# Mixture-of-experts kernel: the block for crowded experts moved ahead of the fourth expert from the end, and gathered columns computed transposed, 192 at once

## The chip, the cores and the metric

The kernel runs on one core of a Trainium2 chip. The metric is device time in microseconds of one execution. A core has five engines with queues of their own: PE (TensorE, matrix products into PSUM), DVE (VectorE), ACT (ScalarE), POOL (GpSimd) and SP (SyncE, which here issues the DMAs). They meet through semaphores.

## The reference, cut to what matters

One encoder layer on 256 tokens of width 1024: three token mixers (attention, a state-space scan, a convolution), a merge, a LayerNorm, then 32 experts, of which each token uses four, and a last LayerNorm. All in float32. The part around the change is the mixture of experts:

```python
logits = t @ router_w + router_b                    # t: 256 x 1024, normalised
top_vals, top_idx = lax.top_k(logits, 4)            # of 32 experts
gates = softmax(top_vals)
# for each expert e, on the tokens that chose it:
h = xe @ w_gu[e] + b_gu[e]                          # 1024 -> 2048
gate, up = minimum(h[:, :1024], 7), clip(h[:, 1024:], -7, 7)
y = ((up + 1) * (gate * sigmoid(1.702 * gate))) @ w_dn[e] + b_dn[e]   # 1024 -> 1024
# output: sum over the token's experts of gate * y; then
x = layernorm(2**0.25 * x + ffn, ln2_g, ln2_b)
```

The weights of the experts, 32 x 12 MB in float32, are read once from HBM.

## The kernel before, in words

**Weights.** Each expert has twelve tiles of 1 MB: eight of `w_gu` (the "up" tiles, one for each 128 rows, index k) and four of `w_dn` (the "down" tiles). They go through a ring of 19 slots in SBUF, in the order of use (`load`, L746 to L751, all on SP's queue). A slot is loaded again when its reader on PE is done. The first 19 tiles are loaded during the mixers, as space comes free (`do_pre`, `open_ring`).

**The chain ahead of the experts** (L1033 to L1110) is an order written out by hand on all engines: the first LayerNorm (`norm`, into `nrm[0]` and `nrm[1]`), the router, ranks of the tokens within each expert, sizes, and the columns of the first two experts (`gather_first`). Then ACT casts the normalised tokens to fp32r (`nh_`), DVE subtracts for the remainder (`nl_`), and POOL prepares the residual sum `acc`. PE multiplies float32 in two instructions and fp32r in one; tokens in fp32r are gathered as the sum of a high and a low part, so nothing is lost.

**An expert** (`expert`, L1224) has two ways of working. Its size class is computed in the kernel (`size`: 0 up to 32 tokens, 1 up to 64, 2 above) and read into registers of the engines, which branch on it. Class 1, here called *large*, uses `up_many`: 64 token columns (`xg`) are the stationary operand, and the weights move in 512 columns. Class 0, *small*, uses `up_four`: 32 columns (`xs_`, a copy of the first 32 of `xg` made by `small_columns` on ACT), with four quarters of the weights side by side in PE's column groups. Class 2, *both*, uses `up_many` for the first 64 tokens and `up_four` for the next 32. For that class alone a branch at the start (L1248) gathers the columns of these 32 tokens into `xs_` with 32 products of 32 columns (L1241) and eight copies. Every expert passes that branch on PE, ACT and DVE. In this execution there are 19 small experts, 10 large ones and three with both (2, 15 and 17); 30 and 31 are large.

After up comes the SwiGLU on DVE and ACT, then transposes, the down products (L1312 for 64 rows, L1343 for 32), the weighing by the gate (`weigh`: `yh` on ACT, `yl` on DVE). The result of an expert is added to the tokens by two scatters (`flush`), which stand between the up products of the next expert; DVE adds them into `acc` (L1205).

**Gathering for a later pair.** Experts are taken in pairs. While an even expert runs, PE gathers the rows of the next pair: eight products of 512 columns (`gather`, L984), with the one-hot as stationary operand, giving 128 token rows in `rawx`. While the odd one runs, PE transposes them eight times (`spread_rows`, L998), and ACT and DVE copy them to `xg` with the LayerNorm's gain and offset (`xcopy`, four copies each). These steps stand in `fill`, between SwiGLU and the down products. PE's order here is written out by hand (`pe_order`); the other engines' order follows the program.

**Experts with more than 96 tokens.** The rest of such an expert's tokens is worked on by `heavy`, in a block (L1439 to L1448) that stands ahead of expert 31, behind that expert's loads. It is a branch on the largest count, and within it one for each of the 32 experts. PE, ACT, DVE and POOL all pass it. `heavy` loads weights again on POOL's queue, into the four slots of the ring that follow the last load (`free`); ahead of expert 31 nothing else is to be loaded after that. Because the result of expert 30 is still waiting for its scatter there, the block has buffers of its own (`rest`). `hint` marks where the code behind the jump may be fetched early.

Of the kernel before, what the change touches and what calls it, by code (L numbers as in the profile page):

```python
# [30 lines left out]
TOP = CAP + TINY  # L31
LIMIT = 7.0
# [149 lines left out]
def tile_trunk(ctx, tc, xT_d, xn_d, wf_d, vec_d, row_d, rw_d, cst_d, cst2_d, rope_d, ln1_d, ln2_d,  # L182
# [697 lines left out]
    x1t = [mo.tile([P, KT, P], F32, tag="xg", name=f"x1t{c}", bufs=2) for c in range(2)]  # L880
    raw = mo.tile([P, D], F32, name="rawx")
    xgx = raw.rearrange("p (k n) -> p k n", k=KT)
# [8 lines left out]
    ohp = [mo.tile([P, 2, 2, CAP], F32R, tag="ohp", name=f"ohp{t}", bufs=2) for t in range(1)]  # L891
# [49 lines left out]
    def choose(c):  # L941
        lg = ch.tile([P, NE], F32, name=f"lg{c}")
# [25 lines left out]
    def gates(c):  # L968
        gq = ch.tile([P, 4, NE], F32, tag="gq", name=f"gq{c}", bufs=1)
# [5 lines left out]
    def onehot(dst, c, e0):  # L975
        V.tensor_tensor(dst[:, c], C("iota_s", 0, CAP).unsqueeze(1).to_broadcast([P, 2, CAP]),
                        rank[c][:, e0:e0 + 2].unsqueeze(2).to_broadcast([P, 2, CAP]), op=ALU.is_equal)
# [9 lines left out]
    def xcopy(dst, src, k):  # L987

        if k >= KT // 2:
# [4 lines left out]
    def spread_rows(dst, src, name):  # L994
        for hf in range(2):
            pT = sm(f"pgt{name}{hf}", [P, 4, P])
            for k in range(4):
                T.transpose(pT[:, k], src(4 * hf + k), C("ident"))  # L998
            for k in range(4):
                xcopy(dst[:, 4 * hf + k], pT[:, k], 4 * hf + k)  # L1000

    def gather_first(c):

        for k in range(KT):
            T.matmul(pgd[k // 4][:, k % 4], nrm[c][:, k * P:(k + 1) * P], pair(ohp[0], c).bitcast(F32),
                     start=(c == 0 and k % 4 == 0), stop=(c == 1 and k % 4 == 3))

    def small_onehot(e):
        ohs = mo.tile([P, 2, TINY], F32R, tag="ohs", name=f"ohs{e}", bufs=2)
        for c in range(2):  # L1010
# [9 lines left out]

    def rowk(k):
        return raw[:, k * P:(k + 1) * P]

    def pair(oh, c):
        return oh[:, c].rearrange("p r s -> p (r s)")

# [580 lines left out]
```

## Time and profile before

| | |
|---|---|
| median of 3 runs | 1365.44 us (1362.12 to 1366.07) |
| the profiled execution, its own time | 1365.53 us |
| its span, first to last instruction | 1363.7 us |
| granted clock of PE, mean over the span | 0.952 of 2.4 GHz |
| PE, DVE, ACT, POOL busy | 84%, 41%, 24%, 12% |
| read from HBM | 453.27 MB, of which the experts 402.7 MB |

The busy shares are means over the whole span. The mixers take about the first 360 us, the chain ahead of the experts lies at about 364 to 387 us, the experts run to about 1345 us, and the last LayerNorm ends the span. A share of DMA above 1 in a window is a rounding of the packets at its edges. A count of matrix products in a row counts instructions: a float32 product has two.

### The profile page before, as it was taken

Reading aid. Unit: us, or ns where it says so; the run is one execution under the profiler, and the core shown is the slowest. Engines: PE = TensorE matmul, PEld = TensorE weight load, DVE = VectorE, ACT = ScalarE, POOL = GpSimd, SP = SyncE. Lnnn points to the kernel's source line nnn. Section 1 sums busy time; section 2 is a strip of 40 time slices with the busy share of each in tenths; the row PEclk is TensorE's granted clock in tenths of the full one; section 3 lists DMA queues with packets and bytes.
Section 4 is the critical chain, followed back from the end, with each engine's and each line's share of the span. In section 5 each row is a group of like instructions: output and inputs, shape, how many; then the busy total and the mean of one; then the engine's idle time right before and its main releaser. Section 6 shows DMA issues by size and latency. Waiting matters only on the chain. (4 is left out here: it accounts for less than half of the span.)

```text
span 1363.7 us, 21824 instructions
## 1 busy us (share of the span) xinstructions
PE 1140.3 (84%) x8035; PEld 595.8 (44%) x8035; DVE 559.5 (41%) x1206; ACT 330.2 (24%) x690; POOL 169.1 (12%) x93
## 2 busy tenths in 40 slices
PE   7999899989978987888888779898888688767875
PEld 6877789889833332322332223232322232212222
DVE  3668888866752323322332222322233222222214
ACT  5666665644421110110010111111111101000101
POOL 3442234457130000000000000000000000000000
PEclk9999899999988999999999899998999999988978
DMA  7334345468879899999999999998999999999991
GB/s 228 124 109 155 124 140 186 155 209 282 313 283 419 344 371 397 418 419 419 417 419 420 419 419 418 420 419 357 387 417 417 419 419 420 418 419 420 418 393 39
DMA packets 73627, 456.47 MB, mean 335 GB/s; under 512 B 8304, under 2 KB 8704, under 8 KB 26752
## 3 DMA queue, kind: packets, MB, share of 16 engines
q1 hardware_dynamic: 73472, 454.35, 83.2%
q8 instruction: 103, 1.69, 0.5%
q14 instruction: 52, 0.43, 0.1%
HBM read 453.27 MB, written 1.05 MB: 333 GB/s over the span
## 5 line engine op out<-in xcount | busy, mean ns | idle before, releaser
L1271 PE MATMUL pGS<-ew,xsm 128*32 128x512 f32 x1408 | 183.8, 627 | 57.4 <-DMA ew<-in_wgu_dram 33.2
L1261 PE MATMUL pGL<-ew,xg 128*64 128x512 f32 x832 | 198.2, 615 | 3.2 <-DMA ew<-in_wgu_dram 2.9
L1205 DVE TENSOR_TENSOR xn<-xn,pos 128x512 f32<-128x512 f32 x124 | 79.8, 684 | 218.1 <-PE pos L1201 218.1
L247 POOL TENSOR_TENSOR wl<-raw,wh 128x1024 fp32r<-128x1024 f32 x56 | 136.8, 2450 | 160.9 <-ACT wh L246 154.6
L1194 DVE SCALAR_TENSOR_TENSOR yl<-pY,gsl,yh 128x512 fp32r<-128x512 f32 x35 | 26.3, 751 | 244.1 <-ACTq L1248 103.3
L1134 ACT ACTIVATE sg<-gv 128x256 f32<-128x256 f32 x48 | 20.0, 417 | 437.5 <-DVE gv L1133 436.7
L1495 POOL TENSOR_TENSOR xn<-xn,lb 128x256 f32<-128x256 f32 x4 | 2.8, 728 | 959.8 <-DVE xn L1483 959.8
L1271 PEld LDWEIGHTS pGS<-ew,xsm 128*32 128x32 f32 x1408 | 44.2, 112 | 156.9 <-issue 93.8
L1343 PE MATMUL pY<-ew,hT 128*32 128x512 f32 x704 | 87.0, 628 | 24.6 <-ACT hT L1329 17.6
L1261 PEld LDWEIGHTS pGL<-ew,xg 128*64 128x64 f32 x832 | 57.4, 140 | 114.3 <-issue 93.5
L246 ACT CAST wh<-raw 128x1024 fp32r<-128x1024 f32 (+1 forms) x89 | 91.1, 1028 | 55.9 <-DMA raw<-in_wf_dram 17.3
L1312 PE MATMUL pY<-ew,hT 128*64 128x512 f32 x416 | 102.2, 648 | 0.0
L1193 ACT ACTIVATE yh<-pY,gsl 128x512 fp32r<-128x512 f32 x35 | 24.1, 687 | 197.0 <-PEq L1316 71.4
L247 DVE TENSOR_TENSOR wl<-raw,wh 128x1024 fp32r<-128x1024 f32 (+1 forms) x33 | 41.5, 1263 | 41.9 <-ACT wh L246 41.9
L1312 PEld LDWEIGHTS pY<-ew,hT 128*64 128x64 f32 x416 | 31.0, 149 | 61.9 <-issue 60.4
L1343 PEld LDWEIGHTS pY<-ew,hT 128*32 128x32 f32 x704 | 20.4, 114 | 75.6 <-issue 33.6
L1267 PE MATMUL pGS<-bgu_t,bl 128*32 128x512 f32 x176 | 26.3, 664 | 28.7 <-DVEq L1248 10.9
L1018 ACT COPY xsm<-xg 128x256 f32<-128x256 f32 x32 | 12.9, 402 | 148.4 <-PE pGS L1271 132.0
L1201 PEld LDWEIGHTS pos<-yh,sc 64*128 64x128 f32 x124 | 12.2, 183 | 56.9 <-issue 56.9
L1325 PE MATMUL pY<-bdn_t,bl 128*32 128x512 f32 x88 | 24.0, 623 | 14.3 <-PEq L1316 14.3
L1201 PE MATMUL pos<-yh,sc 64*128 64x512 f32 x124 | 31.0, 491 | 4.7 <-PEq L1277 4.7
L417 DVE SCALAR_TENSOR_TENSOR xacc<-xp,vec,xacc 128x256 f32<-128x256 f32 x48 | 32.4, 676 | 2.7 <-ACT xacc L415 1.5
(462 smaller groups left out, 2126.2 us busy)
## 6 DMA issues: line engine op xcount, KB each, us to landing
ew<-in_wgu_dram SPq DMA_DIRECT2D x241, 1024.0 KB, 19.9
ew<-in_wdn_dram SPq DMA_DIRECT2D x124, 1024.0 KB, 19.9
raw<-in_wf_dram SPq DMA_DIRECT2D x87, 512.0 KB, 3.6
ew<-in_wgu_dram SPq DMA_DIRECT2D x30, 512.0 KB, 6.3
ew<-in_wdn_dram SPq DMA_DIRECT2D x8, 512.0 KB, 4.6
xraw<-in_xT_dram SPq DMA_DIRECT2D x4, 256.0 KB, 5.8
xn<-in_xn_dram SPq DMA_DIRECT2D x2, 512.0 KB, 5.3
lnt<-in_ln_dram SPq DMA_DIRECT2D x2, 512.0 KB, 10.5
```

Of the source, the lines that this page charges most:

```text
L246: A.copy(h[:, b], raw[:, b])
L247: (PO if u in LOW_POOL else V).tensor_sub(l[:, b], raw[:, b], h[:, b].bitcast(F32))
L417: V.scalar_tensor_tensor(acc, xp[:, j:j + S], W("cw5", t * 5 + j), acc, op0=ALU.mult, op1=ALU.add)
L1193: A.activation(yh, pY, AF.Copy, scale=gsl)
L1194: V.scalar_tensor_tensor(yl, pY, gsl, yh.bitcast(F32), op0=ALU.mult, op1=ALU.subtract)
L1201: T.matmul(pos[n], sc[r, c * P:(c + 1) * P], y[r], start=(start and i == 0), stop=(i == 1))
L1205: V.tensor_add(dst, dst, po)
L1261: T.matmul(pL[q][h * 64:(h + 1) * 64].rearrange("p (g n) -> p g n", g=2), xg[:, k, s_], quarter(wt[k], h, q), start=False, stop=(k == KT - 1))
L1267: T.matmul(grp(pS, g), bl[:, g * TINY:(g + 1) * TINY].bitcast(F32), bgu_t[:, q * 512:(q + 1) * 512].bitcast(F32), start=True, stop=False)
L1271: T.matmul(grp(pS, g).rearrange("p (g n) -> p g n", g=2), xs_[:, k], quarter(wt[k], h, q), start=False, stop=(k == KT - 1))
L1312: T.matmul(pY[0][n * 64:(n + 1) * 64], hT[b][:, j, h * CAP:(h + 1) * CAP], wt[KT + 2 * b + h][:, j, n * 512:(n + 1) * 512], start=False, s ...
L1343: T.matmul(grp(pY, 2 * n + j), hT[:, j, g * TINY:(g + 1) * TINY], w[:, j, n * 512:(n + 1) * 512], start=(j == 1 and (b, h) == (0, 0)), sto ...
```

## The change

1. Columns of a pair are gathered directly in transposed form: the tokens (`nh_`, `nl_`, 128 at a time) are the stationary operand, and a one-hot of 192 columns moves: 64 for each of the two experts, and 32 more for each for the small class. These are 32 products for a pair, sixteen in each expert. The 32-column part is in the one-hot and in `xg` from the start, so `small_columns`, the copies into `xs_`, the branch at the start of an expert and its gather go, except for experts 0 and 1.
2. For experts 0 and 1, whose columns come from `gather_first`, `more_columns` keeps the branch. For expert 0 it stands in the chain, right behind the first copies and ahead of the casts of `nh_`. `gather_first` is cut into halves, and the order of a few steps beside it changes.
3. The block for experts over 96 tokens stands ahead of expert 28, behind the scatter of expert 27, which is taken out of expert 28. It uses the ring's next four tiles, which are those that expert 29 loads first. `rest` and `rawx` go.

```diff
@@ onehots and gather
-    def gather(pg, c, oh, parts=(0, 1)):
-        for i in parts:
-            src = (nh_, nl_)[i]
-            for hf in range(2):
-                T.matmul(pg[hf], oh, src[:, c, hf * 512:(hf + 1) * 512],
-                         start=(c == 0 and i == 0), stop=(c == 1 and i == 1))
+    def onehot_small(dst, c, e):
+        V.tensor_scalar(small(dst, c, e), C("iota_s", 0, TINY), base[:, e:e + 1], rank[c][:, e:e + 1],
+                        op0=ALU.add, op1=ALU.is_equal)
+    def wide(t, c, e):
+        return t[:, c, (e % 2) * CAP:(e % 2 + 1) * CAP]
+    def small(t, c, e):
+        return t[:, c, P + (e % 2) * TINY:P + (e % 2 + 1) * TINY]
+    def gather(dst, oh, k0, name):
+        n = oh.shape[-1]
+        pt = sm(f"pgx{name}{k0}", [P, 2, n])
+        for k in (k0, k0 + 1):
+            for c in range(2):
+                for i, src in enumerate((nh_, nl_)):
+                    T.matmul(pt[:, k - k0], src[:, c, k * P:(k + 1) * P], oh[:, c],
+                             start=(c == 0 and i == 0), stop=(c == 1 and i == 1))
+        for k in (k0, k0 + 1):
+            xcopy(dst(k), pt[:, k - k0], k, k // 2 % 2)
-    def spread_rows(dst, src, name):
...
-    def small_columns(e, xg):
...
+    def more_columns(e, both, pg, rows):
+        with tc.If(both > 1):
+            for k in range(KT):
+                for c in range(2):
+                    for i, src in enumerate(rows):
+                        oh = small(ohp[0], c, e)
+                        l = src[c][:, k * P:(k + 1) * P]
+                        T.matmul(pg[:, k], l, oh.bitcast(F32) if len(rows) == 1 else oh,
+                                 start=(c == 0 and i == 0), stop=(c == 1 and i == len(rows) - 1))
+            for k in range(KT):
+                xcopy(small(xg0, k, e), pg[:, k], k)
@@ chain ahead of the experts
-        first = (ohs0, small_columns(0, xg0))
+        for hf in range(2):
+            gather_first(1, hf)
+            for k in range(4):
+                xcopy(xg0[:, 4 * hf + k, 0:P], pgd[hf][:, k], 4 * hf + k, hf)
+        for e in range(2):
+            A.copy(xg0[:, :, P + e * TINY:P + (e + 1) * TINY], xg0[:, :, e * CAP:e * CAP + TINY])
+            if e == 0:
+                first = sizes(0)
+                more_columns(0, first[2], mm("pgs0", [P, KT, TINY]), (nrm,))
+        T.transpose(prt[:, 1], rank[1], C("ident"))
+        A.copy(rankT[0:NE], prt.rearrange("e c t -> e (c t)"))
         for c in range(2):
             A.copy(nh_[:, c], nrm[c])
@@ def expert
-        ohs, xs_ = first if e == 0 else (small_onehot(e), small_columns(e, xg))
-        pg = bank(5, f"pgs{e}", [P, KT, TINY])
...
-        with tc.If(both > 1):
-            gather_more()
-            copy_more()
+        if e == 1:
+            more_columns(e, both, bank(5, f"pgs{e}", [P, KT, TINY]), ...)
@@ up_four
-                    T.matmul(grp(pS, g).rearrange("p (g n) -> p g n", g=2), xs_[:, k],
+                    T.matmul(grp(pS, g).rearrange("p (g n) -> p g n", g=2), xg[:, k, x_],
@@ loop over the experts
+    LATE = NE - 4
+    def columns(dst, e0):
+        with tc.issue_after(last["ch"].ins):
+            for c in range(2):
+                onehot(dst, c, e0)
+                for i in range(2):
+                    onehot_small(dst, c, e0 + i)
...
-        def fill(arm="", e=e, more=more):
-            if more and e % 2 == 0:
-                pg = [sm(f"pgx{e}{arm}{hf}") for hf in range(2)]
-                for c in range(2):
-                    gather(pg, c, pair(ohn, c))
-                A.copy(raw[:, 0:512], pg[0])
-                V.tensor_copy(raw[:, 512:D], pg[1])
-            elif more:
-                spread_rows(xgn, rowk, f"{e}{arm}")
+        def fill(e=e, more=more):
+            if more:
+                for k0 in (0, 2) if e % 2 == 0 else (4, 6):
+                    gather(lambda k: xgn[:, k], ohn, k0, str(e))
...
-        if e == NE - 1:
-            rest = (mo.tile([P, S], F32R, tag="ohp", name="sch", bufs=2), ...)
+        if e == LATE:
+            flush(prev)
+            prev = None
             free = [nload[0] + i for i in range(4)]
             with tc.If(count(NE, ALL) > TOP, label="overflow"):
                 for x in range(NE):
                     with tc.If(count(x, ALL) > TOP):
                         for part in range(2):
-                            heavy(x, part, [load(x, u, free[u % 4], PO) for u in range(12)], (f"{x}x", *rest))
+                            heavy(x, part, [load(x, u, free[u % 4], PO) for u in range(12)], (f"{x}x", *parked))
```

`heavy` gathers with the same `gather`, and `hint` now stands at expert 27.

## Rows read from the trace of the kernel before

**Rows 1.** Ten-microsecond windows; columns: length, busy times with counts, PEclk, DMA share, GB/s
```profile
380.00:390.00 10.00, 5.39 (x32) 1.55 (x31) 8.87 (x21) 5.71 (x9) 4.22 (x3) 0.83 0.03 10
...
470.00:480.00 10.00, 8.34 (x56) 2.50 (x52) 3.69 (x6) 1.07 (x2) 0.00 (x0) 1.00 0.23 77
...
510.00:520.00 10.00, 6.81 (x54) 2.05 (x50) 2.27 (x4) 0.69 (x1) 0.00 (x0) 1.00 0.74 287
...
930.00:940.00 10.00, 8.32 (x54) 2.67 (x54) 3.69 (x6) 1.07 (x2) 0.00 (x0) 1.00 0.57 231
...
970.00:980.00 10.00, 7.04 (x42) 1.81 (x42) 2.26 (x4) 0.69 (x1) 0.00 (x0) 0.83 0.78 305
...
1330.00:1340.00 10.00, 7.91 (x36) 2.74 (x34) 3.49 (x10) 1.60 (x4) 0.00 (x0) 1.00 0.05 19
```

**Rows 2.** Page, DMA issues: count, KB each, median us from issue to landing
```profile
ew<-in_wgu_dram SPq DMA_DIRECT2D x241, 1024.0 KB, 19.9
```

**Rows 3.** Timeline of PE, first expert: start, us, engine, line, operands, [idle before, releaser]
```profile
378.39 2.47 PE L1005 MATMUL pgd<-ohp,nrm 128*128 128x128 f32 x16
...
386.67 3.42 PE L1271 MATMUL pGS<-ew,xsm 128*32 128x512 f32 x16 [3.88 <-ACTq L1248]
```

**Rows 4.** Timeline of ACT ahead of the first expert
```profile
382.37 0.40 ACT L1018 COPY xsm<-xg 128x256 f32<-128x256 f32 x1 [0.85 <-DVE gs L970]
...
384.57 2.00 ACT L1095 ACTIVATE lnt<-lnt 128x1024 f32<-128x1024 f32 x2
```

**Rows 5.** Timeline of DVE, first expert
```profile
391.11 2.37 DVE L976 TENSOR_TENSOR ohp<-cst,rank 128x128 fp32r<-128x128 f32 x2
396.01 1.50 DVE L1011 TENSOR_SCALAR ohs<-cst,base,rank 128x32 fp32r<-128x32 f32 x2 [2.53 <-PE aux L1144]
```

**Rows 6.** Windows restricted to L1241: PE, PEld, clock, DMA
```profile
432.30:436.00 3.70, 3.60 (x32) 3.60 (x32) 1.00 1.01 421
812.50:816.30 3.80, 3.66 (x32) 3.65 (x32) 1.00 1.01 423
887.70:891.50 3.80, 3.69 (x32) 3.65 (x32) 1.00 1.01 418
```

**Rows 7.** Windows restricted to L984, one of fifteen pairs
```profile
879.30:881.40 2.10, 2.04 (x8) 1.42 (x8) 1.00 1.01 421
```

**Rows 8.** Windows restricted to L998, one of fifteen pairs
```profile
918.50:919.50 1.00, 0.99 (x8) 0.86 (x8) 1.00 1.02 426
```

**Rows 9.** Window of PE over the fp32r products with 256 columns, L290 to L292
```profile
324.81:334.19 9.38, 9.38 (x82) 1.00 0.82 283
```

**Rows 10.** Timeline of PE around expert 15 and the start of expert 16
```profile
811.32 1.06 PE L1343 MATMUL pY<-ew,hT 128*32 128x512 f32 x8 [1.17 <-DMA ew<-in_wdn_dram]
...
847.68 0.70 PE L1305 MATMUL pTL<-cst,uv 128*128 128x128 f32 x2 [2.82 <-ACT hT L1306]
...
867.20 1.06 PE L1267 MATMUL pGS<-bgu_t,bl 128*32 128x512 f32 x8 [0.88 <-ACTq L1248]
```

**Rows 11.** Timeline of PE, start of expert 4
```profile
513.78 1.07 PE L1267 MATMUL pGS<-bgu_t,bl 128*32 128x512 f32 x8 [2.73 <-DVEq L1248]
```

**Rows 12.** Windows over expert 16 (small) and 17 (both products)
```profile
867.20:887.80 20.60, 17.86 (x151) 6.41 (x151) 6.97 (x15) 1.80 (x5) 0.00 (x0) 1.00 1.01 417
...
887.80:942.00 54.20, 49.32 (x299) 18.61 (x295) 15.22 (x38) 7.01 (x18) 0.00 (x0) 0.91 0.92 380
```

**Rows 13.** Timeline of PE, start of expert 28
```profile
1212.47 1.06 PE L1267 MATMUL pGS<-bgu_t,bl 128*32 128x512 f32 x8 [1.15 <-ACTq L1248]
```

**Rows 14.** Timeline of SP: issue of expert 29's eight up tiles
```profile
1222.69 19.06 SPq L750 DMA_DIRECT2D ew<-in_wgu_dram  x8
```

**Rows 15.** Instructions of L1205: count, min/median/max ns
```profile
L1205 DVE TENSOR_TENSOR xn<-xn,pos x124: 679/684/690, 411.2 to 1325.8; 128x512 f32<-128x512 f32 x124
```

**Rows 16.** Timeline of PE, experts 30 and 31
```profile
1296.94 8.78 PE L1312 MATMUL pY<-ew,hT 128*64 128x512 f32 x32
1312.68 1.19 PE L1257 MATMUL pGL<-bgu_t,bl 128*128 128x512 f32 x2 [6.95 <-DVEq L1444]
...
1329.80 3.65 PE L1261 MATMUL pGL<-ew,xg 128*64 128x512 f32 x16
...
1336.94 7.09 PE L1312 MATMUL pY<-ew,hT 128*64 128x512 f32 x32
```

**Rows 17.** Instructions of L1444, the jump over the block: count, ns, first and last start
```profile
L1444 DVEq EVENT_SEMAPHORE  x2: 21/21/21, 1312.5 to 1312.6; - x2
...
L1444 DVEq COMPARE_BRANCH  x1: 85/85/85, 1309.8 to 1309.8; - x1
```

More of the change, by code (lines that the diff above doesn't have):

```diff
@@ L879, in tile_trunk @@
     acc = xn
-    x1t = [mo.tile([P, KT, P], F32, tag="xg", name=f"x1t{c}", bufs=2) for c in range(2)]
-    raw = mo.tile([P, D], F32, name="rawx")
-    xgx = raw.rearrange("p (k n) -> p k n", k=KT)
+    x1t = [mo.tile([P, KT, SL], F32, tag="xg", name=f"x1t{c}", bufs=2)[:, :, 0:P] for c in range(2)]
     blt = mo.tile([P, NE, 2], F32R, name="blt")
@@ L890, in tile_trunk @@
     idr = mo.tile([P, P], F32R, name="idr")
-    ohp = [mo.tile([P, 2, 2, CAP], F32R, tag="ohp", name=f"ohp{t}", bufs=2) for t in range(1)]
+    ohp = [mo.tile([P, 2, SL], F32R, tag="ohp", name="ohp0", bufs=2)]
     chain = ExitStack()
@@ L968, in gates @@
     def gates(c):
[L969 removed]
+        gq = eq[c]
         V.reciprocal(gs[c][:, 1:2], gs[c][:, 1:2])
@@ L1021, in rowk, with gather_first, sizes @@
[L1021 to L1025, printed above, removed]
+    def gather_first(c, hf):
+        for k in range(4):
+            kk = 4 * hf + k
+            T.matmul(pgd[hf][:, k], nrm[c][:, kk * P:(kk + 1) * P], ohp[0][:, c, 0:P].bitcast(F32),
+                     start=(c == 0 and k == 0), stop=(c == 1 and k == 3))
+    def sizes(e):
+        return [nc.values_load(size[0:1, e:e + 1], engines=g, min_val=0, max_val=2,
+                               skip_runtime_bounds_check_because="a sum of two comparisons of a count")
+                for g in ((ENG.PE,), (ENG.Activation, ENG.DVE), (ENG.PE, ENG.Activation, ENG.DVE))]
@@ L1055, in tile_trunk @@
         lnt = ch.tile([P, 2, D], F32, name="lnt")
-        nrm = [raw, ch.tile([P, D], F32, name="nrm")]
+        nrm = [ch.tile([P, D], F32, name=f"nrm{c}") for c in range(2)]
         norm(0)
@@ L1065, in tile_trunk @@
         ranks(0)
+        pn = mm("pn", [P, NE])
+        T.matmul(pn, C("ones"), Pm[0], start=True, stop=False)
         zip_run(choose(1), [lambda: None, lambda: V.tensor_mul(rank[0], Pm[0], prk[0]),
@@ L1075, in tile_trunk @@
         onehot(ohp[0], 1, 0)
-        pn = mm("pn", [P, NE])
-        for c in range(2):
-            T.matmul(pn, C("ones"), Pm[c], start=(c == 0), stop=(c == 1))
-        T.transpose(prt[:, 1], rank[1], C("ident"))
-        gather_first(1)
-        A.copy(rankT[0:NE], prt.rearrange("e c t -> e (c t)"))
+        T.matmul(pn, C("ones"), Pm[1], start=False, stop=True)
+        gather_first(0, 1)
         V.tensor_scalar(base, pn, float(CAP), float(CAP), op0=ALU.is_gt, op1=ALU.mult)
-        few = ch.tile([P, NE], F32, name="few")
+        few = ch.tile([P, NE], F32, tag="lg", name="few", bufs=1)
         V.tensor_scalar(few, pn, float(TINY), None, op0=ALU.is_gt)
@@ L1097, in tile_trunk @@
             gates(c)
+        for c in range(2):
+            onehot_small(ohp[0], c, 1)
         cmx = ch.tile([P, 1], F32, name="cmx")
@@ L1358, in heavy_gather @@
         nm = f"{e}h{part}"
-        pg = [sm(f"pgx{nm}{hf}") for hf in range(2)]
-        for c in range(2):
-            gather(pg, c, ohx[:, c])
-        rows = []
-        for i in range(4):
-            r = ex.tile([P, 256], F32, tag=("gv", "uv")[i % 2], name=f"raw{nm}{i}", bufs=2 + i % 2)
-            (V.tensor_copy if i % 2 else A.copy)(r, pg[i // 2][:, i % 2 * 256:(i % 2 + 1) * 256])
-            rows.append(r)
-        spread_rows(xgx, lambda k: rows[k // 2][:, k % 2 * P:(k % 2 + 1) * P], nm)
+        rows = [ex.tile([P, 2, P], F32, tag=("gv", "uv")[i % 2], name=f"xgx{nm}{i}", bufs=2 + i % 2) for i in range(4)]
+        for k0 in range(0, KT, 2):
+            gather(lambda k: rows[k // 2][:, k % 2], ohx, k0, nm)
+        return rows
     def heavy(e, part, wt, cur):
```

77 lines of the change are left out of this document (23 added, 54 removed).

## The prediction

> **What bounds it now.** I read the windows first, for the DMA share, and then the timeline of PE wherever that share falls. Outside a few stretches the share stands at 1.01 and the stream moves about 419 GB/s; one 1 MB tile then takes 1.0486 MB / 419 GB/s = 2.50 us, and an expert's twelve tiles take 30.0 us. A tile lands 19.9 us after its issue [rows 2], so about eight tiles are under way and the other eleven slots of the ring are slack. The weight stream is the bound, and the time can change only where the stream stands still or after it ends.
>
> It stands still in five places [rows 1]. From 380 to 390 us it moves almost nothing (share 0.03, 9.7 us lost): the ring is full and the first expert hasn't started. From 470 to 520 us two windows lose (1 - 0.23/1.01) x 10 = 7.7 us and 2.7 us; from 930 to 980 us two lose 4.4 and 2.3 us. Each of these pairs lies at the end of an expert that runs both products (experts 2, 15 and 17) and of its neighbours: there PE is late and slots come free late. A small expert occupies PE for 20.6 us and one with both products for 54.2 us [rows 12], against 30.0 us of stream, so a cluster with such an expert overruns the slack. I call experts 0 to 3 cluster A and experts 15 to 18 cluster B. In both, a microsecond less on PE is a microsecond less of standing stream, up to what is lost there.
>
> The end is the fifth place. The window from 1330 us has a share of 0.05, so the last tile lands at about 1331 us [rows 1], yet the last down product starts at 1336.94 and takes 7.09 us, to 1344.0 [rows 16]. Before expert 31, PE stands for 6.95 us until DVE has jumped over the block for experts over 96 tokens [rows 16]; DVE branches at 1309.8 and signals at 1312.5 [rows 17]. No instruction of the block itself appears in the trace: no expert has more than 96 tokens, and only the jump is paid.
>
> **The start of expert 0.** PE begins its products at 386.67 after 3.88 us of waiting for ACT to reach the branch at L1248 [rows 3]. On ACT the two casts of nh and the two products for lnt (to 386.57) stand between the small copy, done at 382.77, and that branch [rows 4]. In the new order the branch comes right behind the copies. I add one more small copy (0.4 us) and take a start about 3.4 us earlier. Not all of it stays. The gather in expert 0 now needs the one-hots for all 192 columns, and these stand behind the same DVE work: two wide ones at 391.11 (2.37 us), then four small ones at 1.50 us for two, which makes 2.37 + 3.0 = 5.4 us, ready at about 396.5 [rows 5]. PE, having started early, waits there, and what follows on PE and DVE gains about 1 us. The bounds are 0 and 3.4 us; I take 1.0, because the DVE chain is the nearer row.
>
> **The extra gather of the experts with both products.** It goes for experts 2, 15 and 17: 32 products each, 3.60, 3.66 and 3.69 us of PE [rows 6], with nothing on PE beside them. Expert 2 (cluster A) gains 3.6. Expert 15 had just waited 1.17 us for a tile [rows 10], so part of its early start meets a tile that is not there yet: 3.0, and expert 17 gives 3.6. The bounds are 0, if the stream is what those experts wait for, and the full length.
>
> **The gather for two experts.** Before, it is eight products of 512 columns (2.04 us, in the even expert) and eight transposes (0.99 us, in the odd one) [rows 7, 8], 3.0 us for a pair. After, it is 32 fp32r products of 192 columns for a pair, sixteen in each expert. The trace has such products at 32 columns, 3.60/32 = 0.113 us apart [rows 6], and at 256 columns, 9.38/82 = 0.114 us apart [rows 9]. With 192 in between I take 0.114: 16 x 0.114 = 1.83 us, which is 0.2 less in an even expert and 0.85 more in an odd one. No row lets it be cheaper than 0.113. The upper bound is that 192 columns run like plain f32: eight f32 products of 128 columns take 2.47 us, 0.31 each [rows 3], hence 32 x 0.31 = 9.9 us a pair. Two odd experts in each cluster: +1.7 us for each cluster.
>
> **Branches and copies.** From expert 2 on, no expert begins with a branch on its size. PE waited for it 0.88 us at expert 16 [rows 10] and 2.73 us at expert 4 [rows 11], where DVE's earlier branches are part of the wait. I take 0.4 us (bounds 0 and 0.9) at three starts in each cluster, 1.2 us. The copies of gathered columns lie beside PE, except that in an odd expert they stand on ACT ahead of hT: 2.82 us of PE idle in expert 15 [rows 10]. Two of four such copies leave the odd expert and go to the even one. I count 0.5 us in A and 1.0 in B, with bounds of 0 and twice that. The small copy of columns and the 64 small one-hots are off PE's path in both versions; in steady state the stream covers them.
>
> **The block.** Ahead of expert 28, PE first does expert 27's scatter alone. Its four adds on DVE cost 4 x 0.684 = 2.7 us [rows 15], and the jump costs about the same 6.95 us, so expert 28 starts at about 1212.5 + 9.7 - 1 = 1221 [rows 13], with its tiles waiting in the ring. It is small and needs 20.6 of 30.0 us [rows 12], so it is done at about the time at which it ends now. Behind the block on SP stand the next four tiles, the first four of expert 29, which now also wait until PE and POOL are past it. They are issued from 1222.69 on [rows 14]: in time, and up to some 17 us of lateness would be covered by the eight tiles under way. If that cover is gone, each further microsecond is a microsecond of stream.
>
> The profile's row shows the stall once, at 1312.68 [rows 16]. The Trainium skill (Runtime: NRT & Kernel Launch, "Instruction fetch mechanics") says that a taken branch to code that is not loaded waits for that code to be fetched by DMA; by it the stall moves with the block and doesn't shrink, which the single jump of this trace agrees with. By the rule a stall with no slack around it would be paid in full at expert 28.
>
> What the move gives back is at the end. Expert 31 starts at about 1306 instead of 1312.68, so its up products follow the tiles. Its last up tile lands four tiles before the end, at 1331 - 10 = 1321, and is used by 1323. From the end of up (1329.80 + 3.65 = 1333.45) to the start of down (1336.94) it takes 3.5 us now [rows 16], so down runs from 1326.5 to 1333.6. That is 10.4 us before 1344.0. If PE's clock has dropped, down takes 8.78 us as in expert 30 [rows 16], which leaves 8.7. I take 8.5, with bounds of 6 and 10.4.
>
> **Sum.** A: -1.0 - 3.6 + 1.7 - 1.2 - 0.5 = -4.6. B: -3.0 - 3.6 + 1.7 - 1.2 - 1.0 = -7.1, of which the stream can take at most the 4.4 + 2.3 = 6.7 lost there; I take 5.5. End: -8.5. Together -18.6 us. The profiled execution took 1365.53 us, 1.8 more than its span of 1363.7 and 0.1 above the median of 1365.44. The forecast is 1365.5 - 18.6 = 1347 us, and its own range is 1338 to 1355: all bounds on the good side give about -27, and the weak ones (A nothing, B 3, end 7) -10.
>
> **Rivals.**
> *Narrow fp32r products run at the plain f32 price* (chance 0.19). For it: no row of this trace has one between 32 and 256 columns, and 32 columns may sit on a floor that hides a slow rate. Against: the two neighbours agree at 0.113 and 0.114. It adds 9.9 - 3.0 = 6.9 us a pair, 3.4 an expert. Cluster A then changes by -4.6 - 1.7 + 4 x 3.4 = +7.3, B by -7.1 - 1.7 + 13.6 = +4.8, and the end still gives -8.5: 1369 us. Between the clusters PE catches up 9.4 us in a small expert; with 3.4 more everywhere it may not, and 19 x 3.4 = 65 us less the 11 of the extra gathers, 5 of branches and about 16 of waiting for tiles makes +33, hence 1390. I give 1380. It decides from the point at which a pair costs more than about 5 us.
>
> *The clusters gain nothing* (0.10): the stream is the bound and early PE work only waits for tiles. For it: the share of 1.01 nearly everywhere. Against: the four windows where it stood while PE worked. Only the end remains: 1357 us.
>
> *The stall is paid at the new place* (0.06): the four tiles or expert 28 come later than the slack allows. With a jump of 30 us the tiles would be released near 1215 + 30 = 1245, 5 us past the 17 us of cover: 1352.
>
> *The move and the gather cancel* (0.05): a product at about 0.2 us eats both clusters and part of the end, within 0.3% of before.
>
> **Chances.** Forecast 0.60, the others as given. A difference under 0.3% (4 us) can't be told from none here. Faster by more: 0.60 + 0.10 + 0.06 = 0.76. Slower: 0.19 less its lower edge, 0.17. Same: 0.05 and that edge, 0.07. The range of 1338 to 1367 takes in the likeliest case and its weaker neighbours and leaves most of the first rival outside.
>
> **What would show it.** Right: sixteen products of 192 columns about 0.114 us apart; first product of expert 0 near 383; no gather of 32 columns at 430, 812 and 888; windows of the two clusters at a share near 1; no long idle of PE before expert 31, one of about 9 us before expert 28 with the stream at 1.01 beneath it; the last down product ending some 3 us after the last tile. Wrong: products 0.2 to 0.3 us apart, with the low windows longer and more of them; or a stream that stands near 1220 to 1250.

## The result, and the profile after

The changed kernel took 1345.66 us (median of 4 runs, 1343.39 to 1346.01) beside 1365.76 us for the kernel before (4 runs, 1362.12 to 1368.19): a ratio of 0.985 with a 95% interval of 0.9829 to 0.9871. That is 20.1 us less; 18.6 were forecast.

**One clock for all runs.** Up to the copy that ACT makes of expert 0's 32 columns [rows 4 for before] the kernels differ in the order of a few steps only, yet in the profiles here that copy starts anywhere from 379.8 to 390.3 us. Below, positions are therefore counted from it and given as a difference to the kernel before. Three are used: when the 50,000th of the 73,472 packets of the weights' queue lands (between the clusters), when the 60,000th does (after cluster B), and when the last down product ends. Kernels that share a stretch agree in it to some 0.3 us. The copy itself started 2.6 us earlier in the profiled execution after (379.81 against 382.37). Of this, 2.4 us arise ahead of the router's first product (366.91 and 364.47), in the mixers, whose code the change leaves alone; they are taken for chance. The rest is the change:

| | stream after A | stream after B | last down product |
|---|---|---|---|
| forecast, cumulated | -4.6 | -10.1 | -18.6 |
| measured | -5.5 | -13.6 | -20.0 |
| by part, forecast | A -4.6 | B -5.5 | end -8.5 |
| by part, measured | A -5.5 | B -8.1 | rest -6.4 |

The windows after answer to [rows 1]; columns as there.

```profile
380.00:390.00 10.00, 7.63 (x85) 2.47 (x85) 9.70 (x21) 4.69 (x7) 5.26 (x4) 1.00 0.58 211
...
460.00:470.00 10.00, 8.79 (x44) 2.93 (x40) 2.38 (x4) 0.69 (x1) 0.00 (x0) 1.00 0.54 224
470.00:480.00 10.00, 9.08 (x58) 2.84 (x59) 2.42 (x6) 1.07 (x2) 0.00 (x0) 1.00 0.73 272
...
930.00:940.00 10.00, 9.29 (x53) 4.83 (x53) 4.26 (x12) 2.51 (x6) 0.00 (x0) 1.00 1.01 418
...
970.00:980.00 10.00, 8.62 (x91) 3.00 (x87) 3.41 (x7) 0.00 (x0) 0.00 (x0) 1.00 1.01 418
...
1310.00:1320.00 10.00, 8.00 (x37) 2.88 (x35) 3.33 (x9) 1.60 (x4) 0.00 (x0) 1.00 0.39 159
```

Cluster B loses nothing any more (every window from 800 to 1000 us has a share of 1.01 or 1.02); cluster A still does, at 460 to 480. Next, PE's rows after: expert 0 (against [rows 3]); a product of the gather, the wait for hT and the down products of expert 15 (against [rows 9, 10]); the new place of the block; and expert 31 (against [rows 16]).

```profile
380.97 1.92 PE L1272 MATMUL pGS<-ew,xg 128*32 128x512 f32 x16 [0.73 <-ACTq L1024]
...
391.89 0.33 PE L998 MATMUL pgx<-ohp,nh 128*128 128x192 f32 x1 [0.31 <-DVEq L1290]
...
397.48 0.48 PE L1329 MATMUL pTS<-cst,uv 128*128 128x128 f32 x2 [1.96 <-DVEq L1301]
398.57 5.05 PE L1344 MATMUL pY<-ew,hT 128*32 128x512 f32 x32 [0.62 <-ACT hT L1330]
...
832.37 0.27 PE L998 MATMUL pgx<-ohp,nh 128*128 128x192 f32 x1
832.48 0.27 PE L998 MATMUL pgx<-ohp,nl 128*128 128x192 f32 x1
...
834.48 0.51 PE L1306 MATMUL pTL<-cst,uv 128*128 128x128 f32 x2 [0.56 <-ACT hT L1307]
834.91 7.09 PE L1313 MATMUL pY<-ew,hT 128*64 128x512 f32 x32
...
1204.41 1.93 PE L1268 MATMUL pGS<-bgu_t,bl 128*32 128x512 f32 x8 [2.27 <-PEq L1276]
1206.10 3.65 PE L1272 MATMUL pGS<-ew,xg 128*32 128x512 f32 x16
...
1292.94 0.70 PE L1258 MATMUL pGL<-bgu_t,bl 128*128 128x512 f32 x2 [1.86 <-DVEq L1317]
1293.57 3.65 PE L1262 MATMUL pGL<-ew,xg 128*64 128x512 f32 x16
...
1314.43 7.09 PE L1313 MATMUL pY<-ew,hT 128*64 128x512 f32 x32
```

Products of 192 columns start 0.11 us apart, so the first rival fell. The wait for hT is 0.56 us where it was 2.82. Expert 31 waits 1.86 us where it was 6.95, and its products run without a wait for tiles from 1293.57 on: at the end, PE is the bound. It is so by little: the last tile lands at 1318.5, and the last down product ends at 1321.5, 3.0 us later, as the prediction had said.

### The profile page after: what moved, and what is told of

The parts are those of the page before. It is cut to its first block, busy times and chain, and to the rows that moved or that the text cites. A ratio compares the mean times of both kernels' runs of the same rounds, so it can differ in the third digit from the quotient of the medians.

```text
span 1341.6 us, 21767 instructions
## 1 busy us (share of the span) xinstructions
PE 1140.8 (85%) x8179; PEld 603.1 (45%) x8179; DVE 547.8 (41%) x1179; ACT 311.8 (23%) x633; POOL 168.4 (13%) x93
## 3 DMA queue, kind: packets, MB, share of 16 engines
q1 hardware_dynamic: 73472, 454.35, 84.6%
## 5 line engine op out<-in xcount | busy, mean ns | idle before, releaser
L1272 PE MATMUL pGS<-ew,xg 128*32 128x512 f32 x1408 | 193.3, 652 | 60.0 <-DMA ew<-in_wgu_dram 41.2
L1272 PEld LDWEIGHTS pGS<-ew,xg 128*32 128x32 f32 x1408 | 43.0, 113 | 165.6 <-DMA ew<-in_wgu_dram 61.3
L1313 PE MATMUL pY<-ew,hT 128*64 128x512 f32 x416 | 92.1, 595 | 0.0
L1211 ACT ACTIVATE yh<-pY,gsl 128x512 fp32r<-128x512 f32 x35 | 24.1, 687 | 187.9 <-PEq L1317 67.0
L998 PEld LDWEIGHTS pgx<-ohp,nh 128*128 128x128 f32 x240 | 48.5, 202 | 34.2 <-issue 19.4
L998 PE MATMUL pgx<-ohp,nh 128*128 128x192 f32 x240 | 61.2, 297 | 3.1 <-DVE xn L1223 1.5
L998 PE MATMUL pgx<-ohp,nl 128*128 128x192 f32 x240 | 58.4, 283 | 0.0
L1288 DVE COPY gsl<-aux 128x2 f32<-128x2 f32 x32 | 5.1, 158 | 116.8 <-PEq L1276 62.3
L998 PEld LDWEIGHTS pgx<-ohp,nl 128*128 128x128 f32 x240 | 48.6, 203 | 0.0
L1268 PE MATMUL pGS<-bgu_t,bl 128*32 128x512 f32 x176 | 24.4, 622 | 21.9 <-DVEq L1323 13.2
## 6 DMA issues: line engine op xcount, KB each, us to landing
ew<-in_wdn_dram SPq DMA_DIRECT2D x124, 1024.0 KB, 19.9
lnt<-in_ln_dram SPq DMA_DIRECT2D x2, 512.0 KB, 10.5
```

What stands on the lines that cost most here:

```text
L998: T.matmul(pt[:, k - k0], src[:, c, k * P:(k + 1) * P], oh[:, c], start=(c == 0 and i == 0), stop=(c == 1 and i == 1))
L1211: A.activation(yh, pY, AF.Copy, scale=gsl)
L1268: T.matmul(grp(pS, g), bl[:, g * TINY:(g + 1) * TINY].bitcast(F32), bgu_t[:, q * 512:(q + 1) * 512].bitcast(F32), start=True, stop=False)
L1272: T.matmul(grp(pS, g).rearrange("p (g n) -> p g n", g=2), xg[:, k, x_], quarter(wt[k], h, q), start=False, stop=(k == KT - 1))
L1313: T.matmul(pY[0][n * 64:(n + 1) * 64], hT[b][:, j, h * CAP:(h + 1) * CAP], wt[KT + 2 * b + h][:, j, n * 512:(n + 1) * 512], start=False, s ...
```

## The experiments

Each ran beside the kernel before (medians of 1365.5 to 1366.9 us there). Positions are those defined above; each comes from one profiled execution. Counted against the change, the medians agree with the last down product within 2 us, but for three kernels: a_e0late is 10.8 us later by medians and 6.2 by position, a_extra_act 17.0 and 13.6, a_gather 15.8 and 20.0. Sizes taken from these three are less sure.

| kernel | stream after A | after B | last down | median, us | ratio (95% interval) |
|---|---|---|---|---|---|
| the change | -5.5 | -13.6 | -20.0 | 1345.66 | 0.985 (0.9829 to 0.9871) |
| a_block31 | -5.7 | -13.7 | -13.2 | 1353.69 | 0.991 (0.9883 to 0.9936) |
| b_block28 | -0.1 | -0.2 | -6.7 | 1360.08 | 0.996 (0.9938 to 0.9982) |
| a_noblock | -5.4 | -13.4 | -19.5 | 1347.50 | 0.9865 (0.9833 to 0.9897) |
| a_extra | +0.9 | -4.7 | -7.6 | 1356.14 | 0.9926 (0.9899 to 0.9952) |
| a_branch | -5.8 | -13.8 | -17.4 | 1347.33 | 0.9857 (0.9826 to 0.9888) |
| a_e0late | -1.0 | -9.1 | -13.8 | 1356.50 | 0.9933 (0.9900 to 0.9966) |
| a_order | -9.5 | -17.5 | -20.1 | 1345.99 | 0.9848 (0.9814 to 0.9882) |
| a_twice | -5.2 | -12.5 | -17.7 | 1349.81 | 0.9874 (0.9843 to 0.9906) |
| a_gather | +11.5 | +5.7 | 0.0 | 1361.45 | 0.9968 (0.9944 to 0.9991) |
| a_best | -9.6 | -17.5 | -24.1 | 1343.33 | 0.9835 (0.9805 to 0.9865) |
| a_block3 | +10.0 | +2.2 | -3.9 | 1360.46 | 0.9948 (0.9929 to 0.9967) |
| a_extra_act | +4.1 | +1.3 | -6.4 | 1362.61 | 0.997 (0.9955 to 0.9985) |

### The block: back at the end, moved alone, left out, and in cluster A

```diff
a_block31, a_block3 (the change with)
-    LATE = NE - 4
+    LATE = NE - 1        # a_block3: LATE = 3
b_block28 (before with)
-        if e == NE - 1:
-            rest = (...)
+        if e == NE - 4:
+            flush(prev)
+            prev = None
...                        # heavy(..., *parked), hint at NE - 5
a_noblock (the change with)
-        if e == LATE:     # and all of the block
```

> The changed kernel with its block put back ahead of expert 31 (behind the scatter of expert 30), the gather as changed. Theory (end and clusters are separate terms): expert 31 starts after the scatter alone and the jump, some 4 + 6.6 us later than in the changed kernel, and the end pays 8.5 to 10.5 us of it: 1354 to 1356 us; the stream up to the last tile is as in the changed kernel, so the last tile lands at the same place within 1 us. Rival (the gather made nearly all of the gain, the end was covered by the stream): under 3 us, at most 1349. Rival (the block's place made all of it): back to 1364 or more.

> The kernel before with only the block moved ahead of expert 28 (scatter of expert 27 ahead of it, the parked buffers in place of its own). Theory: the end gains 7 to 10 us, the two clusters lose as before: 1355.5 to 1358.5 us, windows at 470 to 520 and 930 to 980 us as low as before. Rival (the move only works where the gather has made PE early): within 2 us of before. Rival (the stall is paid at expert 28): the stream stands there near 1215 to 1250 us and the time is 1360 or more. Together with the changed kernel's block put back, the two parts should add to the 20 us measured, within 2 us.

> The changed kernel without the block for experts over 96 tokens; what it leaves out is the work for such tokens, of which this data has none. Theory: the stall of PE ahead of expert 28 (6.6 us) and the scatter alone lie under the stream, so nothing is left to gain: 1344 to 1346.5 us. Rival (the stall is paid at the new place): 6 us or more less, at most 1340.

> The changed kernel with its block ahead of expert 3, in cluster A, right behind expert 2, where the stream stands still because PE is late. Theory (the jump costs PE the same everywhere, and what lies around it decides): PE stands 6 to 7 us there and does expert 2's scatter alone, and the stream after cluster A is 6 to 10 us later; 1351 to 1356. Rival (the stall is small or hidden anywhere but at the end, because loads run ahead by eight tiles): under 2 us.

Put back, the block costs 6.8 us at the last down product (-13.2 for -20.0) and nothing in the stream; moved alone, it gives 6.7. The two add up to the whole within 0.1 us (-13.2 - 6.7 = -19.9), so place and gather are separate terms. By medians the sum is -17.2 of 20.1; these carry the spread ahead of the copy. The size is below what was expected of both (8.5 to 10.5, and 7 to 10). The median of b_block28, 1360.08, even reaches the 1360 of its rival (the stall is paid at expert 28), but that rival's sign is missing: the DMA share is 1.01 or more from 1215 to 1255 us, and the last tile lands 1.0 us earlier behind the copy than before. PE's rows in a_block31 show its make-up: expert 31 starts behind the scatter alone and the jump, and its first sixteen products run at a lower clock (4.94 us for 3.65). At the jump PE waits 1.57 us; the 6.6 expected for it are the whole stretch from expert 27 to expert 28 in the change (1197.8 to 1204.41), so the scatter was counted twice.

```profile
1302.17 1.19 PE L1258 MATMUL pGL<-bgu_t,bl 128*128 128x512 f32 x2 [1.57 <-DVEq L1441]
1303.29 4.94 PE L1262 MATMUL pGL<-ew,xg 128*64 128x512 f32 x16
```

Left out, the block gives nothing (-19.5 for -20.0, though expert 28 then starts 6.1 us earlier; the median, 1347.50, is 1 us above what was expected): at expert 28 the stall is hidden. In cluster A it isn't. There it costs 15.5 us of stream, above the expected 6 to 10. PE stands and does expert 2's scatter alone, as expected, but SP stops too, because the four tiles behind the block are in its queue. SP's rows and two windows of a_block3:

```profile
441.75 11.67 SPq L751 DMA_DIRECT2D ew<-in_wdn_dram  x4
483.91 9.14 SPq L751 DMA_DIRECT2D ew<-in_wgu_dram  x8
```

```profile
460.00:470.00 10.00, 9.48 (x55) 4.85 (x53) 3.29 (x9) 2.10 (x5) 0.00 (x0) 1.00 0.00 2
470.00:480.00 10.00, 7.28 (x50) 2.07 (x46) 3.69 (x6) 1.76 (x3) 0.00 (x0) 1.00 0.01 3
```

From 453.4 to 483.9 us SP issues nothing, and what was under way runs out. PE itself stands 6.3 us between experts 2 and 3 (479.1 to 485.41). This is the rival "the stall is paid at the new place", real at a place without slack.

The Trainium skill (Runtime: NRT & Kernel Launch, "Instruction fetch mechanics") says that a taken branch to code that is not loaded waits until that code is fetched. The prediction took from it that the stall moves and doesn't shrink. With the gather as before, PE's wait at the jump bears that out. The row of expert 28 in b_block28:

```profile
1224.68 1.94 PE L1267 MATMUL pGS<-bgu_t,bl 128*32 128x512 f32 x8 [6.09 <-PEq L1275]
```

That is 6.09 us for 6.95, and expert 28 starts 9.9 us later than before, where 9.7 were priced. In the changed kernels the jump shrank: PE waits 2.27 us in the change, 1.57 in a_block31 and 1.97 in a_block3. No run shows why. In a_block3 the tiles queued behind the jump cost more than PE's standing.

### Branch and extra gather

```diff
a_extra (the change with)
-        if e == 1:
+        if e >= 1:
             more_columns(e, both, ...)   # writes the same columns again
a_branch (a_extra with)
-        with tc.If(both > 1):
+        with tc.If(both > (1 if e < 2 else 2)):
```

> The changed kernel with the branch on the size at the start of every expert from 1 on and, in experts 2, 15 and 17, the gather of 32 columns and its eight copies put back; they write again what is there already. Theory: 3.6 us of PE for each of the three, most of it one for one at expert 2 and part of it at 15 and 17 (that cluster no longer loses, so it has some slack), and 0.4 to 0.9 us for the branch in late starts: 6 to 11 us, so 1351.5 to 1356.5. Rival (the standing stream there came from something else, such as copies on ACT or the old row gather): under 2 us, at most 1348.

> The changed kernel with the branch on the size put back at the start of every expert from 2 on, over a body that no expert takes: the branch alone, without the 32 products. With branch, gather and copies put back the stream was 5.6 us later after cluster A and 2.2 us more after B, and the last down product 11.6 us later. Theory (the branch is a term of its own, priced at 1.2 us per cluster in the prediction): 1 to 2.5 us at A, 0 to 1 at B, 0 to 3 at the end, together 2 to 5 us: 1348 to 1351. Rival (the 32 products and their copies are all of it): within 1 us of the changed kernel. Rival (the branch is most of it): 7 us or more.

With both put back the stream is 6.4 us later after A and 2.6 us more after B (-4.7 - 0.9 = -5.6 in B, for -8.1). With the branch alone it is not later anywhere, where 1 to 2.5 us were expected in A. So the branches' 1.2 us per cluster were not there; in the stream, the 32 products and their copies are all of it. In B they count for little, since B without them has slack left. At the end a_branch is 2.6 us later, but expert 31 waits the same 1.86 us; its down products in experts 29 and 30 take 5.27 and 8.52 us, where the change has 3.84 (2.78 + 1.06) and 7.09.

### Expert 0

```diff
a_e0late (the change with)
-            if e == 0:
-                first = sizes(0)
-                more_columns(0, ...)
...
             A.mul(lnt[:, i], lnt[:, i], DN_ALPHA)
+        first = sizes(0)
+        more_columns(0, ...)
a_order (the change with)
-        lnt = ch.tile(...)
         nrm = [ch.tile(...) for c in range(2)]
+        lnt = ch.tile(...)
...      # and sg, gv, uv are the first tiles of the pool "ex", over nrm[0]
```

> The changed kernel with the branch of expert 0 back behind the casts of nh and the products for lnt on ACT, as before. Theory (the prediction's, 1.0 of 3.4 us kept): expert 0's first product 3.4 us later, but expert 2 starts at most 1 us later, since expert 0 then waits less for the columns and for POOL; time 0 to 1 us more, at most 1347. Rival (the start is kept one for one): the stream after cluster A is 3.4 us later and the time 1349.

> The changed kernel with one thing more: the SwiGLU tiles of expert 0 lie in memory that POOL has long read (nrm of the first 128 tokens) instead of memory that it reads last, so DVE's gv of expert 0 no longer waits 3.74 us for POOL. Theory (a microsecond of PE in cluster A is a microsecond of stream as long as that cluster still loses some 8 us at 460 to 510): expert 0's down products and everything to expert 3 come 3 to 3.7 us earlier, the stream after A 2.5 to 3.7 us earlier, time 1342 to 1343.5. Rival (another wait, on DVE's columns or ACT, takes its place): under 1 us.

The late branch costs 4.5 us of stream in A: against the change, the start is kept one for one, and more. The theory, which was the prediction's, fell. Against the kernel before, though, nothing of the early start is left two experts later. The last product of expert 1 ends 50.1 us behind the copy before, 50.3 in the change and 54.2 in a_e0late. This is its row before; that of the change is shown further down:

```profile
427.05 5.41 PE L1343 MATMUL pY<-ew,hT 128*32 128x512 f32 x32 [0.53 <-ACT hT L1329]
```

From expert 0's first product to that point PE takes 45.8 us before and 49.2 in the change. So the rest of the change costs 3.4 us in experts 0 and 1, and the early start pays for it.

In a_order the stream gains another 4.0 us in A, a little more than expected. DVE's rows of expert 0, first of the change, then of a_order:

```profile
390.28 1.46 DVE L982 TENSOR_SCALAR ohp<-cst,base,rank 128x32 fp32r<-128x32 f32 x2
395.48 0.42 DVE L1151 TENSOR_SCALAR gv<-pGS 128x256 f32<-128x256 f32 x1 [3.74 <-POOL xn L1128]
```

```profile
392.65 0.42 DVE L1154 TENSOR_SCALAR gv<-pGS 128x256 f32<-128x256 f32 x1 [0.33 <-DVEq L1293]
394.72 0.42 DVE L1156 TENSOR_SCALAR uv<-pGS 128x256 f32<-128x256 f32 x1 [1.64 <-POOL xn L1127]
```

The wait of gv is gone, but the next instruction, uv, now waits 1.64 us for POOL, as the rival had it in part: the down products of expert 0 start only 1.2 us earlier (17.6 us behind the copy for 18.8). The rest comes in expert 1. Its down products in the change, the window around them, and the same products in a_order:

```profile
424.27 5.84 PE L1344 MATMUL pY<-ew,hT 128*32 128x512 f32 x32 [0.62 <-ACT hT L1330]
```

```profile
424.00:428.00 4.00, 3.73 (x20) 0.99 (x24) 0.00 (x0) 0.22 (x1) 0.00 (x0) 0.50 1.01 416
```

```profile
423.22 3.64 PE L1347 MATMUL pY<-ew,hT 128*32 128x512 f32 x32 [0.56 <-ACT hT L1333]
```

The granted clock was 0.50 there, the lower of its two levels, and 1.00 in a_order. Yet the last down product gained 0.1 us, and the median, 1345.99, misses the 1342 to 1343.5 expected: the last experiment shows why.

### The gather: doubled, alone, and with the wait for hT put back

```diff
a_twice (the change with)
-        for k in (k0, k0 + 1):
+        for k in (k0, k0, k0 + 1, k0 + 1):     # each product twice
a_gather (a_extra with the late branch of a_e0late)
a_extra_act (a_extra with, in odd experts)
-            xcopy(dst(k), pt[:, k - k0], k, k // 2 % 2)
+            for _ in range(2):
+                xcopy(dst(k), pt[:, k - k0], k)   # all on ACT, twice
```

> The changed kernel with each product of the column gather issued twice (the first result is overwritten): 16 more products of 0.111 us, 1.8 us of PE, in each expert to the thirtieth. Theory (PE time counts in the clusters only, less the slack that B now has, about 5 us): four experts in A make 5 to 7 us, B 2 to 5, the small experts between nothing, the end 0 to 2: 7 to 13 us, so 1353 to 1359. Rival (gather products lie beside other waits): under 3 us. Rival (PE is the bound everywhere): 30 x 1.8 = 53 us.

> The changed kernel with the branch and the extra gather of experts 2, 15 and 17 put back and the branch of expert 0 back behind the casts of nh: the transposed gather of 192 columns alone, and the block at expert 28. By the prediction's terms (gather +1.7, copies -0.5 and -1.0) the stream should be 1.2 us later than before after cluster A and 0.7 us more after B. Theory now (in B the odd experts' wait for hT, 2.8 us before and 0.6 after, and the clock that PE then keeps are the gain, not the gather): A +1 to +5, depending on whether the start of expert 0 adds to the rest, and B -5 to -6; time 1355 to 1360. Rival (the gain in B needs the extra gather gone): B within 1.5 us of none.

> The kernel with branch and extra gather put back, and in odd experts all four copies of gathered columns on ACT, each issued twice: 3.6 us of ACT ahead of hT in place of 0.9. It asks whether the odd experts' wait for hT (2.8 us before, at experts 15 and 17) and the clock that falls behind it are what the transposed gather gained in cluster B (5.6 us with the extra gather kept). Theory: PE waits 2 to 3 us for hT in experts 15 and 17 again, the granted clock falls to half in their down products (8.8 us in place of 7.1), and B gains only 0 to 2 us against before; last down product some 4 us later than without these copies, 1359 to 1361. Rival (the gain in B is the PE time of the gather itself): B still gains 4 us or more, and the time stays at 1356.

Doubled, the gather adds 30 x 16 x 0.111 = 53 us to PE's work, and the last down product comes 2.2 us later (4.2 by medians), the stream 0.3 after A and 1.1 after B: a miss, far below 7 to 13. Expert 2 even starts 3.4 us earlier than in the change, although DVE's wait for POOL is still there (3.78 us). The added products stand where PE would have waited, and the clock holds: it is 1.00 from 388 to 444 us, where the change falls to 0.50.

Alone (a_gather), the profiled execution was the slowest of twelve and has low clocks in experts 0 and 1, so that its +11.5 in A is not to be read. Its B is: 11.5 to 5.7, a gain of 5.8 us with the extra gather still there. The prediction's own terms said +0.7. (The median of 1361.45 is above the 1355 to 1360 expected.) The windows over expert 15 show where it comes from: before, in a_extra and in the change.

```profile
816.20:867.20 51.00, 45.68 (x265) 14.91 (x265) 14.47 (x37) 6.76 (x17) 0.00 (x0) 0.90 1.01 420
```

```profile
826.30:873.80 47.50, 44.30 (x275) 15.52 (x278) 13.20 (x32) 6.92 (x18) 0.00 (x0) 0.95 1.01 420
```

```profile
804.60:850.70 46.10, 42.32 (x270) 14.74 (x270) 14.09 (x34) 4.81 (x11) 0.00 (x0) 1.00 1.01 420
```

From before to a_extra PE loses idle time (5.3 to 3.2 us), and over the three its clock comes back (0.90, 0.95 and 1.00, the number ahead of the DMA share). The down products of expert 15 before, which stand behind the wait of 2.82 us for hT:

```profile
848.32 9.86 PE L1312 MATMUL pY<-ew,hT 128*64 128x512 f32 x32
```

9.86 us for what takes 7.09 after. With the wait put back (a_extra_act), the rows of experts 15 and 17 are:

```profile
856.63 0.70 PE L1312 MATMUL pTL<-cst,uv 128*128 128x128 f32 x2 [2.88 <-ACT hT L1313]
857.26 8.28 PE L1319 MATMUL pY<-ew,hT 128*64 128x512 f32 x32
...
929.53 0.51 PE L1312 MATMUL pTL<-cst,uv 128*128 128x128 f32 x2 [2.88 <-ACT hT L1313]
929.97 7.09 PE L1319 MATMUL pY<-ew,hT 128*64 128x512 f32 x32
```

The wait is back in both, the lower clock in one of two, and B's gain falls from 5.6 to 2.8 us (4.1 to 1.3). So the wait and the clock behind it are about half of what the gather gains in B with the extra gather kept. No run isolates the other half, but its size is not strange: with the wait back, the two groups of down products still take 4.4 us less than before (8.28 + 7.09 for 9.86 + 9.88), as the clock fell less.

PE and stream can be compared directly. From the end of cluster A (the stream's position there) to the last down product of expert 17, PE gains 2.5 us against before in a_extra_act, 6.2 in a_extra and 17.8 in the change; in B the stream gains 2.8, 5.6 and 8.1. That is one for one until all that stood is gone.

How often does the clock fall behind such a wait? Odd experts whose down products have 64 rows wait 2.1 to 2.9 us for hT five times before and five times in a_extra_act. Behind four of the first five and two of the others the 32 products take longer than 7.09 us (8.20 to 9.88). Of the 23 such groups behind waits under 0.9 us, in these two kernels and the change, none does. So the fall goes with waits of this length without being certain behind them, and they aren't its only cause: a_order, below, has it in experts 30 and 31 behind the waits that the change has there. The Trainium skill (TensorE: Matmul & The Clock Gate, "HAM oscillation — how this bites in real kernels") says that where bursts of products alternate with waits for data, the next burst starts at the lower clock; the rows of a_extra_act agree for expert 15 and don't for 17.

### A version that keeps PE at work

```diff
a_best (a_order with)
+    in experts 0, 1 and 24 to 29: each gather product twice, as in a_twice
         def fill(e=e, more=more):
             if more:
...
+            else:
+                pt = sm(f"pidle{e}", [P, SL])
+                for i in range(10):
+                    T.matmul(pt, nh_[:, 0, 0:P], oh[:, 0], start=(i == 0), stop=(i == 9))
```

> The kernel with expert 0's SwiGLU tiles off POOL's memory, and with PE kept at work where its clock fell: gather products issued twice in experts 0, 1 and 24 to 29, and ten products that nothing reads between up and down of experts 30 and 31. Theory (with the tiles moved the stream was 3.9 us earlier and the end gave it back through PE at half clock, 1.8 + 1.7 + 1.3 us of longer down products in experts 29, 30 and 31): PE stays at 1.00 from 1240 us on, the last down product ends 3 to 5 us earlier than in the changed kernel, 1341 to 1343. Rival (experts 30 and 31 bound the end by their waits for SwiGLU and branches, whatever the clock): within 1 us of the changed kernel. Rival (the added products cost their own time): 1 us or more later.

a_order had its stream 3.9 us earlier than the change, and lost it in the last experts, whose down products had run at 7.09 us in the change. Its down products of experts 30 and 31, and then those of a_best:

```profile
1281.29 8.78 PE L1316 MATMUL pY<-ew,hT 128*64 128x512 f32 x32
...
1313.55 8.41 PE L1316 MATMUL pY<-ew,hT 128*64 128x512 f32 x32
```

```profile
1284.04 7.09 PE L1316 MATMUL pY<-ew,hT 128*64 128x512 f32 x32
...
1311.14 1.33 PE L1437 MATMUL pidle<-ohp,nh 128*128 128x192 f32 x10 [0.15 <-PEq L1281]
...
1314.40 7.09 PE L1316 MATMUL pY<-ew,hT 128*64 128x512 f32 x32
```

With PE busy in the gap between up and down, both run at full clock, and the last down product ends 4.1 us earlier than in the change, as expected. One window at 1245 us still shows 0.51. The median is 1343.33 us (1340.93 to 1346.61), 0.9835 of before. That the version beats the change rests on one profile of each, counted from the copy; the intervals of the medians overlap (0.9805 to 0.9865, and 0.9829 to 0.9871).

## Why the prediction was right, and which of its steps failed

The mechanism was right: the stream is the bound, it stands still where PE is late, and the end is a separate term. That the total came within 1.5 us (18.6 for 20.1) is in part luck: errors of terms cancelled, and the clock of PE in the clusters, which turned out to matter, has no term in the sum.

- **Products of 192 columns**: 0.114 forecast, 0.11 measured.
- **Start of expert 0**: first product 3.1 us earlier behind the copy (4.30 to 1.16), 3.4 forecast. Of this, 1.0 was to be kept; by the end of expert 1 nothing is (50.1 before, 50.3 after). The reason given failed too: the columns on DVE hold PE up by 0.31 us in expert 0 of the change, not for the length of the early start. What was not foreseen is DVE's wait of 3.74 us for POOL, of which PE waits 1.96, and the lower clock behind it (5.05 us for expert 0's down products, 3.64 before). Against the change the start is worth its full length (a_e0late); the rest of the change costs as much in experts 0 and 1.
- **Extra gather and branches in A**: -3.6 - 1.2 = -4.8 forecast, -6.4 measured (a_extra). Of the branches' share, nothing was found (a_branch).
- **Copies in A**: -0.5 forecast. At expert 3 the wait for hT went from 2.14 to 0.61 us, 1.5 less.
- **Cluster B**: forecast from PE at -7.1 and capped. PE's stretch from the start of expert 15 to the start of expert 18 shortened by 14.9 us (125.8 to 110.9), twice as much, and the stream took 8.1, all that stood still. The failed step is the term for the copies of gathered columns, "0.5 us in A and 1.0 in B": the wait for hT went from 2.82 and 2.68 to 0.56 us at two experts, and their down products from 9.9 to 7.1, 5.0 us for each expert beside the 3.7 of the extra gather.
- **The two lows of [rows 1] in B as a cap**: about right; 8.1 us came where 6.7 were read in them.
- **The block at expert 28**: hidden, and SP's tiles in time, as forecast (a_noblock). PE's standing there was priced at 9.7 us. Moved alone, the block costs 9.9 (b_block28); in the change 6.1, against the kernel without the block, because the jump shrank.
- **The end**: -8.5 forecast, -6.7 measured. The step that failed is the last tile's landing, read as 1331 from the share of a window. It is issued at 1312.7 and lands 20.8 us later, at 1333.5. Its row of DMA issues before, and the first sixteen up products of expert 31:

```profile
ew<-in_wdn_dram SPq DMA_DIRECT2D x1, 1024.0 KB, 20.8
...
1313.80 5.80 PE L1261 MATMUL pGL<-ew,xg 128*64 128x512 f32 x16
```

The later landing leaves 2.5 us less to gain: 7.9 for 10.4 and 6.2 for 8.7, by the prediction's own working. What was gained is 5.1 us of waiting ahead of expert 31 (6.95 to 1.86) and 2.2 us in these products, which had a granted clock of 0.62 before and take 3.65 us after. "Its up products follow the tiles" is nearly right: in the change no up product of expert 31 waits for a tile, but the last up tile lands at 1308.4 and the last up product ends at 1311.0, 2.6 us behind it, for 2 forecast.

That the terms don't simply add within a cluster shows in A: -4.5 for the start and -6.4 for the extra gather are more than the -5.5 measured. Each was taken away from the full change, and each brings back waits and a lower clock beside its own time. PE's ends of experts, behind the copy and against before, show where the 5.5 come from: +0.2 us at expert 1, -3.2 at expert 2 (its extra gather is gone) and -5.2 at expert 3 (its wait for hT is 1.5 shorter).

## What to carry to other kernels

Where a transfer stream is the bound, price an edit by the stretches where the stream stands, and there count what it does to PE's waits between bursts too, since products behind such a wait may run at the lower clock. A rare block costs what lies around it: ahead of small experts with a full ring it was free, at the end it cost 6.7 us, and in a cluster that was late 15.5, where PE stood 6.3 us for it and the loads queued behind it stopped for 30.5. A term measured by taking it out of the changed kernel need not be its share of the gain over the old one: the early start was worth 4.5 us one way and nothing the other. Once the stream is hurried, look again at the end: there 3.9 us of stream were worth 0.1 us until PE kept its clock.

## What the runs showed of the chip that was not expected

- Adding 480 matrix products, 53 us at 0.111 us each, to PE's 1141 us busy cost 2.2 us (4.2 by medians; the busy time rose by 40), and expert 2 came earlier by it. The granted clock around expert 1 was 1.00 with them and 0.50 without.
- The same 32 down products take 7.09 us at 2.4 GHz and up to 9.88 where the clock fell to 1.2 GHz for a part of them. Before, 9.86 and 9.88 stood behind waits of 2.82 and 2.68 us; in the change all thirteen such groups run at 7.09.
- Kernels with the same mixers reach expert 0's copy between 379.8 and 390.3 us, one profile of each. That is of the size of the spread between runs of one kernel (1359.6 to 1373.1 us in 23 runs of the kernel before); whether it is the same spread, no run shows.
